# RWKV output stage: two products per token tile are made in the early rounds, parked in DRAM, and loaded when the tile is finished

## The chip, the cores and the metric

The kernel runs on one core of one Trainium2 chip. TensorE (PE) multiplies, VectorE (DVE), ScalarE (ACT) and GpSimd (POOL) work on elements, SyncE (SP) issues most of the DMAs, and ACT and POOL issue some. The metric is the device time of one execution in microseconds (us), as the median of the runs; lower is better.

## The reference, cut to what matters

A two-layer encoder for 512 + 256 = 768 tokens of width 1024. Half of the first layer's mixer is bidirectional RWKV-7 with 8 heads of 64. What is changed computes its last step, for each token, from the two scans' sum `y`:

```
y = scan_forward + scan_backward                          # (tokens, 8 heads, 64)
y = (y - mean(y)) * rsqrt(var(y) + 64e-5)                 # per head
y = y * lnx_w + lnx_b
bonus = sum(r * 0.5 * (k_f + k_b) * r_k) * v              # one number per head and token, times v
out_b = (y + bonus) * g
```

So out_b = yn * (lnx_w * g) + (lnx_b + bonus) * g, where yn is the normalised y. Only yn needs the scans. The result goes, beside the attention half, into the output projection, and from there into the post-norm, the FFN and the second layer.

## The kernel before, in words

The 768 tokens are six tiles of 128 rows (`NT = 6`). `v`, `g`, and the operands of the scan are made first and parked in DRAM (`park`). The scan is cut into chunks of 64 tokens; `Core.rwkv` returns `rounds(lo, hi)`, whose loop variable `n` runs over 24 steps, one chunk of one direction each, forward and backward by turns.

In step `n` the loop fetches step `n+3` (`ahead`: KB, RH, AL, SUV, Ti, all issued by SP), runs `chain` (the part that carries the state S: PE, ACT, PE, ACT and DVE, PE, and two DVE operations on S), and runs `prep` for step `n+2` (PE products, masked by DVE into LR and LK, lines 990 and 1001). When both directions have passed both chunks of a tile, `finish(t)` runs: it is called at n = 10, 11, 14, 15, 22 and 23 for tiles 2, 1, 3, 0, 5 and 4. It loads `v` into `z` (tag gz) and `g` (tag gq), normalises `y`, and applies weight, bias, bonus and gate; PE transposes `z`, and ACT and DVE split it into the operand pair of the output projection. Tags gz and gq have one buffer each; the square of `y` also sits in gq.

Steps 0 to 9 run inside the phase of the differential attention, whose matmuls, softmax and small POOL operations (lines 885 to 887) share the engines with them. Steps 10 to 23 run after it, beside the splitting of the output projection's weights (`wo`: cast on ACT, line 139, difference on POOL, line 140). The output projection follows in `out_and_norm`; its first results need the post-norm's weights (`mix_post`, line 179), which are loaded into space that the recurrence's pool gives back.

The order on each engine isn't written out by hand: a planner puts the instructions in order by priority and by its own simulation, and every queue then runs in that order. `rank(100)` moves `chain` ahead in priority, `rank(-60)` moves `prep` back, and matmuls with operands of type float32r are fillers. A load can be issued long before its place in the program if its buffer is free.

Of the kernel before, what the change touches and what calls it, by code (L numbers as in the profile page):

```python
# [13 lines left out]
ALU = mybir.AluOpType  # L14
# [4 lines left out]
P = 128  # L19
D = 1024  # L20
T = 768
NT = 6
# [32 lines left out]
class Core:  # L55
# [881 lines left out]
    def rwkv(self, rw, park, out):  # L937

        nc, A = self.nc, self.A
        am = []  # L940
        for d in "fb":
            t = rw.tile([P, P], I32, tag="am" + d, name="am" + d)
            nc.scalar.dma_start(t, A["am" + d])
            am.append(t)
        lw, lb = (rw.tile([P, 512], F32, tag=n, name=n) for n in ("lw", "lb"))
        nc.scalar.dma_start(lw, A["lnx_w"].partition_broadcast(P))
        nc.scalar.dma_start(lb, A["lnx_b"].partition_broadcast(P))
        tile = lambda tag, shape, bufs=1: rw.tile(shape, F32, tag=tag, name=self.uid(tag), bufs=bufs)
# [30 lines left out]
        def prep(di, c):  # L979

            u = ready[di, c]
            LK, LR, KBT = (tile(n, [P, 4, 2, 64], NB - 1) for n in ("LK", "LR", "KBT"))
            u["LK"], u["LR"], u["KBT"] = LK, LR, KBT
            KB, RH, AL = (u[n] for n in ("KB", "RH", "AL"))
            st = lambda x, j: x[:, j].rearrange("p s t -> p (s t)")
            b = self.bank("pp")
            for j in range(4):
                self.mm(b[:, j * P:(j + 1) * P], st(KB, j), RH[:, j])
            v = b.bitcast(I32).rearrange("p (j x) -> p j x", x=64)
            nc.vector.tensor_tensor(out=LR.rearrange("p j h x -> p (j h) x").bitcast(I32), in0=v,  # L990
                                    in1=am[di][:, 64:P].unsqueeze(1).to_broadcast([P, 8, 64]), op=ALU.bitwise_and)
            for par in range(2):
                rr = rows[par]
                nc.scalar.copy(out=LK[rr, :, par], in_=AL[rr])
            b = self.bank("pp")
            for j, par in heads:
                self.mm(b[rows[1 - par], j * 64:(j + 1) * 64], KB[rows[par], j, 1 - par], AL[rows[par], j])
            v = b[:, 0:256].bitcast(I32).rearrange("p (j x) -> p j x", x=64)
            for par in range(2):
                rr = rows[par]  # L1000
                nc.vector.tensor_tensor(out=LK[rr, :, 1 - par].bitcast(I32), in0=v[rr],
                                        in1=am[di][rr, 0:64].unsqueeze(1).to_broadcast([64, 4, 64]), op=ALU.bitwise_and)
            b = self.bank("pt")
            for j in range(4):
                self.tr(b[:, j * P:(j + 1) * P], st(KB, j))
            nc.scalar.copy(out=KBT.rearrange("p j h v -> p (j h v)"), in_=b)

        def chain(di, c, first, last):
# [38 lines left out]
                nc.scalar.copy(out=ys[o, c // 2], in_=yb[o])  # L1047
            done.add(c)

        def finish(t):  # L1050

            y = ys[:, t]
            hv = lambda x: x.rearrange("p (h v) -> p h v", h=8)
            bc = lambda x: x.unsqueeze(2).to_broadcast([P, 8, 64])
            st = tile("gst", [P, 3, 8], 2)
            z, q = (tile(n, [P, 512]) for n in ("gz", "gq"))
            nc.sync.dma_start(z, park["v"][t * P:(t + 1) * P])
            nc.vector.tensor_reduce(out=st[:, 0], in_=hv(y), axis=AX.X, op=ALU.add)
            nc.vector.tensor_scalar(out=st[:, 0], in0=st[:, 0], scalar1=1.0 / 64, scalar2=None, op0=ALU.mult)
            nc.vector.tensor_tensor(out=hv(y), in0=hv(y), in1=bc(st[:, 0]), op=ALU.subtract)  # L1060
            nc.scalar.activation(out=q, in_=y, func=AF.Square)
            nc.vector.tensor_reduce(out=st[:, 1], in_=hv(q), axis=AX.X, op=ALU.add)
            self.rpow(st[:, 2], st[:, 1], 1.0 / 64, 64e-5)
            g = tile("gq", [P, 512])
            nc.sync.dma_start(g, park["g"][t])
            nc.vector.tensor_tensor(out=hv(z), in0=hv(z), in1=bc(self.bon[:, t]), op=ALU.mult)
            nc.vector.tensor_tensor(out=z, in0=z, in1=lb, op=ALU.add)
            nc.vector.tensor_tensor(out=hv(y), in0=hv(y), in1=bc(st[:, 2]), op=ALU.mult)
            nc.vector.tensor_tensor(out=y, in0=y, in1=lw, op=ALU.mult)
            nc.vector.tensor_tensor(out=z, in0=y, in1=z, op=ALU.add)  # L1070
            nc.vector.tensor_tensor(out=z, in0=z, in1=g, op=ALU.mult)
            b = self.bank("tr")
            for j in range(4):
                self.tr(b[:, j * P:(j + 1) * P], z[:, j * P:(j + 1) * P])
            out(t, b)
# [4 lines left out]
        def ahead(n):  # L1080
            if n < len(todo):
                fetch(*todo[n])
                fetch_inverse(*todo[n])

        def rounds(lo, hi):
            for n in range(2 * lo, 2 * hi):
                if n == 0:
                    for i in range(3):
                        ahead(i)
                    prep(*todo[0])  # L1090
                    prep(*todo[1])
                di, c = todo[n]
                ahead(n + 3)
                with self.rank(100):
                    chain(di, c, n // 2 in (0, 8), n // 2 in (7, 11))
                if n + 2 < len(todo):
                    with self.rank(-60):
                        prep(*todo[n + 2])
                t = c // 2
                passed[t] = passed.get(t, 0) + 1  # L1100
                if passed[t] == 4:
                    finish(t)
# [248 lines left out]
def body(ctx, tc, A):  # L1351
    nc = tc.nc
    C = Core(ctx, tc, A)
    dp = ctx.enter_context(tc.tile_pool(name="dp", bufs=1, space=DRAM, reuse_waits="tile"))
    park = {}
    for n, shp in (("v", [T, 512]), ("o", [4, P, T]), ("g", [NT, P, 512]), ("AL", [2, 12, P, 4, 64]), ("RH", [2, 12, P, 4, 64]), ("KB", [2, 12, P, 4, 2, 64]),
                   ("Ti", [2, 12, P, 4, 64]), ("x", [NT, P, D]), ("va", [NT, P, 512])):
        park[n] = dp.tile(shp, F32, tag="pk" + n, name="pk" + n)
    C.stats = dp.tile([3, T, 8], F32, tag="stats", name="stats")
    C.vperm = dp.tile([2, T, 256], F32, tag="vperm", name="vperm")  # L1360
# [308 lines left out]
```

## Time and profile before

| | |
|---|---|
| median of 3 runs | 2100.59 us (2097.37 to 2102.23) |
| profiled execution, its own time | 2108.94 us |
| span of that execution, first to last instruction | 2107.1 us |
| busy: PE / DVE / ACT / POOL | 2040.0 / 1393.5 / 904.6 / 867.2 us |
| recurrence beside the attention | about 482 to 597 us |
| recurrence after the attention | about 597 to 697 us |
| last `finish` | 697 to 717 us |
| mean granted clock of TensorE | 0.973 of full speed |

A timeline row gives start, duration, engine, line, operation, output and inputs; in brackets stands how long the engine had been idle before, and what it waited for. A window row gives the busy time of each engine in a stretch (with the count of instructions), the granted clock (1.00 is full speed, 2.4 GHz; 0.50 is 1.2 GHz), the mean busy share of the DMA engines, and GB/s.

### The profile page before, as it was taken

How to read it: one execution, taken by the hardware profiler on the slowest of the kernel's cores; microseconds unless marked ns; L12 is line 12 of the kernel's file. 1: busy time of each engine (PE TensorE's matmuls, PEld its weight loads, DVE VectorE, ACT ScalarE, POOL GpSimd, SP SyncE). 2: the span in 40 equal slices, each digit the busy share in tenths (PEclk: the TensorE clock that was granted, in tenths of full speed). 3: DMA queues.
4: the chain of work that ended last, by engine and by line, in shares of the span. 5: the costliest groups of instructions: out<-in, count | busy, mean ns of one | idle time of the engine just before them, and what ended most of it. 6: DMA issues, size and time to landing. Idle time of an engine off the chain costs nothing. (4 is left out here: it accounts for less than half of the span.)

```text
span 2107.1 us, 33782 instructions
## 1 busy us (share of the span) xinstructions
PE 2040.0 (97%) x13294; PEld 1774.0 (84%) x13294; DVE 1393.5 (66%) x2165; ACT 904.6 (43%) x1703; POOL 867.2 (41%) x819
## 2 busy tenths in 40 slices
PE   7999999999999999999999999999998999999998
PEld 7767777877887788999999998888687999999997
DVE  5456987966579577566666658644568566666665
ACT  5466565367554254433333335222444433333332
POOL 3344332652114137443444535453127435543442
PEclk9999997998999999999999999999899999999999
DMA  4334335114365311211222145221131221211124
GB/s 157 85 76 90 88 80 166 35 34 137 86 184 164 121 74 61 80 61 60 66 85 71 63 147 177 82 82 38 52 110 61 80 80 61 80 61 61 60 80 150
DMA packets 150227, 189.01 MB, mean 90 GB/s; under 512 B 95926, under 2 KB 107784, under 8 KB 150068
## 3 DMA queue, kind: packets, MB, share of 16 engines
q1 hardware_dynamic: 126880, 168.00, 26.1%
q10 hardware_dynamic: 20372, 12.03, 2.0%
q0 software_dynamic: 2816, 6.83, 1.0%
q8 instruction: 104, 1.70, 0.3%
q14 instruction: 55, 0.45, 0.1%
HBM read 150.20 MB, written 36.23 MB: 88 GB/s over the span
## 5 line engine op out<-in xcount | busy, mean ns | idle before, releaser
L83 PE MATMUL gm<-xh,w 128*128 128x384 f32 x864 | 237.2, 338 | 2.9 <-DVE sil L340 2.9
L140 DVE TENSOR_TENSOR wl<-wraw,wh 128x1024 fp32r<-128x1024 f32 (+1 forms) x96 | 131.1, 1366 | 152.7 <-ACT wh L139 150.2
L83 PE MATMUL gm<-T,w 128*128 128x384 f32 x1080 | 212.0, 339 | 6.9 <-DVE w L140 3.0
L83 PE MATMUL gm<-xh,wh 128*128 128x256 f32 (+3 forms) x640 | 207.4, 347 | 0.8 <-ACT pad L503 0.8
L83 PE MATMUL gm<-xl,wh 128*128 128x256 f32 (+3 forms) x640 | 205.7, 346 | 0.0
L83 PE MATMUL gm<-xh,wl 128*128 128x256 f32 (+3 forms) x640 | 204.0, 345 | 0.0
L83 PEld LDWEIGHTS gm<-T,w 128*128 128x128 f32 x1080 | 191.8, 188 | 12.7 <-DVE w L140 4.3
L140 DVE TENSOR_TENSOR w<-S,w 128x512 fp32r<-128x512 f32 x174 | 172.7, 992 | 41.3 <-ACT w L139 31.9
L139 ACT CAST wh<-wraw 128x1024 fp32r<-128x1024 f32 (+1 forms) x103 | 107.5, 1045 | 167.8 <-PE gm L83 104.4
L139 ACT CAST w<-S 128x512 fp32r<-128x512 f32 x174 | 107.8, 621 | 150.7 <-POOL S L299 53.6
L139 ACT CAST w<-wraw 128x512 fp32r<-128x512 f32 x126 | 76.1, 619 | 209.3 <-PE gm L83 139.2
L83 PEld LDWEIGHTS gm<-xh,w 128*128 128x128 f32 x864 | 159.2, 189 | 7.8 <-DVE sil L340 3.5
L83 PE MATMUL sc<-xh,w 128*128 128x384 f32 x544 | 151.3, 339 | 3.5 <-DVE xl L140 2.0
L303 POOL TENSOR_TENSOR S<-wraw,S 128x512 f32<-128x512 f32 x42 | 62.2, 1481 | 204.9 <-DVE w L140 204.9
L83 PE MATMUL gm<-xl,w 128*128 128x384 f32 x432 | 145.8, 338 | 0.0
L140 DVE TENSOR_TENSOR w<-wraw,w 128x512 fp32r<-128x512 f32 x126 | 118.3, 954 | 40.2 <-ACT w L139 39.9
L83 PEld LDWEIGHTS gm<-xh,wh 128*128 128x128 f32 (+1 forms) x640 | 119.2, 193 | 21.5 <-issue 6.1
L83 PEld LDWEIGHTS gm<-xl,wh 128*128 128x128 f32 (+1 forms) x640 | 118.7, 194 | 20.4 <-issue 7.9
L83 PEld LDWEIGHTS gm<-xh,wl 128*128 128x128 f32 (+1 forms) x640 | 118.6, 193 | 20.6 <-issue 7.2
L406 DVE TENSOR_TENSOR acc<-acc,ob 128x512 f32<-128x512 f32 x128 | 87.5, 683 | 64.0 <-PE ob L83 63.0
L358 POOL TENSOR_TENSOR sil<-sil,v 128x384 f32<-128x384 f32 x44 | 46.8, 1065 | 167.1 <-DVE v L340 166.8
L83 PE MATMUL ob<-wl,hh 128*128 128x512 f32 x288 | 113.4, 394 | 0.0
(521 smaller groups left out, 5292.6 us busy)
## 6 DMA issues: line engine op xcount, KB each, us to landing
wraw<-in_gate SPq DMA_DIRECT2D x44, 512.0 KB, 3.4
wraw<-in_down SPq DMA_DIRECT2D x44, 512.0 KB, 3.8
wraw<-in_up SPq DMA_DIRECT2D x40, 512.0 KB, 3.5
wraw<-in_wqk SPq DMA_DIRECT2D x20, 512.0 KB, 3.6
wraw<-in_wo SPq DMA_DIRECT2D x14, 512.0 KB, 3.9
wraw<-in_wrkv SPq DMA_DIRECT2D x12, 512.0 KB, 3.5
KB<-pkKB SPq DMA_DIRECT2D x24, 256.0 KB, 3.3
pkx<-x SPq DMA_DIRECT2D x12, 512.0 KB, 4.7
```

The lines of the kernel that those rows point to most:

```text
L83: return self.nc.tensor.matmul(o, a, b, start=start, stop=stop)
L139: self.nc.scalar.copy(out=hi, in_=x)
L140: (eng or self.nc.vector).tensor_tensor(out=lo, in0=x, in1=hi.bitcast(F32), op=ALU.subtract)
L303: eng.tensor_tensor(out=s2, in0=a12, in1=s2, op=ALU.subtract)
L358: nc.gpsimd.tensor_tensor(out=o, in0=o, in1=a[0], op=ALU.mult)
L406: nc.vector.tensor_tensor(out=accs[t][:, fs], in0=accs[t][:, fs], in1=os[t, f], op=ALU.add)
```

## The change

A new function `gated(t)` is called in steps 4 to 9 for tiles 0 to 5. It loads `v` and `g` of the tile, makes z = (v * bonus + lnx_b) * g and g = g * lnx_w in four DVE operations, and stores both to DRAM from POOL's queue. `finish` loads these two instead of `v` and `g`; three of its DVE operations go (v times bonus, plus bias, and the last multiplication by the gate), and the multiplication by `lnx_w` takes the loaded product. Both functions use tags gz and gq, which keep one buffer each.

```diff
+        def gated(t):
+            z, g = tile("gz", [P, 512]), tile("gq", [P, 512])
+            nc.sync.dma_start(z, park["v"][t * P:(t + 1) * P])
+            nc.sync.dma_start(g, park["g"][t])
+            nc.vector.tensor_tensor(out=hv(z), in0=hv(z), in1=bc(self.bon[:, t]), op=ALU.mult)
+            nc.vector.tensor_tensor(out=z, in0=z, in1=lb, op=ALU.add)
+            nc.vector.tensor_tensor(out=z, in0=z, in1=g, op=ALU.mult)
+            nc.gpsimd.dma_start(park["zg"][t], z)
+            nc.vector.tensor_tensor(out=g, in0=g, in1=lw, op=ALU.mult)
+            nc.gpsimd.dma_start(park["lg"][t], g)
         def finish(t):
...
-            nc.sync.dma_start(z, park["v"][t * P:(t + 1) * P])
+            nc.sync.dma_start(z, park["zg"][t])
...
-            nc.sync.dma_start(g, park["g"][t])
-            nc.vector.tensor_tensor(out=hv(z), in0=hv(z), in1=bc(self.bon[:, t]), op=ALU.mult)
-            nc.vector.tensor_tensor(out=z, in0=z, in1=lb, op=ALU.add)
+            nc.sync.dma_start(g, park["lg"][t])
             nc.vector.tensor_tensor(out=hv(y), in0=hv(y), in1=bc(st[:, 2]), op=ALU.mult)
-            nc.vector.tensor_tensor(out=y, in0=y, in1=lw, op=ALU.mult)
+            nc.vector.tensor_tensor(out=y, in0=y, in1=g, op=ALU.mult)
             nc.vector.tensor_tensor(out=z, in0=y, in1=z, op=ALU.add)
-            nc.vector.tensor_tensor(out=z, in0=z, in1=g, op=ALU.mult)
...
+                if 4 <= n < 4 + NT:
+                    gated(n - 4)
```

## Rows read from the trace of the kernel before

**Rows 1.** Section 1 of the page: busy time, share of span, instructions.

```profile
PE 2040.0 (97%) x13294; PEld 1774.0 (84%) x13294; DVE 1393.5 (66%) x2165; ACT 904.6 (43%) x1703; POOL 867.2 (41%) x819
```

**Rows 2.** Windows, three stretches: PE, PEld, DVE, ACT, POOL, clock, DMA share, GB/s.

```profile
500.00:597.00 97.00, 94.72 (x1300) 79.48 (x1300) 59.42 (x142) 60.30 (x163) 15.85 (x49) 1.00 0.41 115
597.00:680.00 83.00, 75.59 (x1221) 66.52 (x1220) 76.54 (x129) 42.84 (x90) 28.42 (x18) 0.94 0.66 191
680.00:720.00 40.00, 37.43 (x283) 30.32 (x282) 20.16 (x34) 7.18 (x18) 6.18 (x7) 0.99 0.19 59
```

**Rows 3.** View of tile gz: ns min/median/max of one, first and last start.

```profile
L1066 DVE TENSOR_TENSOR gz<-gz,bon x6: 674/681/693, 510.6 to 712.6; 128x512 f32<-128x512 f32 x6
L1067 DVE TENSOR_TENSOR gz<-gz,lb x6: 682/692/2727, 512.8 to 713.3; 128x512 f32<-128x512 f32 x6
L1071 DVE TENSOR_TENSOR gz<-gz,gq x6: 682/691/694, 630.7 to 714.8; 128x512 f32<-128x512 f32 x6
```

**Rows 4.** Timeline of DVE: one of the removed operations.

```profile
638.22 2.73 DVE L1067 TENSOR_TENSOR gz<-gz,lb 128x512 f32<-128x512 f32 x1
```

**Rows 5.** Timeline of POOL beside the first of these.

```profile
638.02 2.37 POOL L140 TENSOR_TENSOR wl<-wraw,wh 128x1024 fp32r<-128x1024 f32 x1
```

**Rows 6.** Timeline of PE, 597 to 680 us: the four longest idle gaps.

```profile
608.46 1.13 PE L84 MATMUL gm<-RH,KB 128*128 128x128 f32 x8 [1.03 <-DMA RH<-pkRH]
...
619.46 0.68 PE L84 MATMUL ob<-SUV,KBT 128*64 128x64 f32 x14 [1.66 <-DVE SUV L1029]
...
649.28 0.33 PE L84 MATMUL sc<-SUV,LK 128*64 128x64 f32 x2 [1.21 <-ACT SUV L1017]
...
665.45 0.65 PE L87 MATMUL tr<-ident,gz 128*128 128x128 f32 x4 [1.17 <-DVE gz L1071]
```

**Rows 7.** Waits, 597 to 672 us: total us, times, longest.

```profile
ACT SUV L1017 <- DVE S L1036: 7.5, 3, 5.1
```

**Rows 8.** Windows of 5 us around the low clock.

```profile
645.00:650.00 5.00, 3.62 (x71) 3.11 (x67) 4.97 (x9) 1.15 (x3) 1.19 (x1) 1.00 0.53 157
650.00:655.00 5.00, 4.73 (x46) 3.95 (x44) 4.86 (x9) 4.23 (x9) 2.58 (x2) 0.66 0.52 150
...
665.00:670.00 5.00, 3.77 (x42) 3.10 (x43) 4.55 (x10) 4.22 (x10) 1.79 (x2) 0.76 0.54 125
670.00:675.00 5.00, 5.00 (x64) 4.66 (x63) 3.42 (x7) 0.79 (x3) 0.13 (x1) 0.55 0.61 178
```

**Rows 9.** Timeline of DVE, the last finish.

```profile
712.61 0.69 DVE L1066 TENSOR_TENSOR gz<-gz,bon 128x512 f32<-128x512 f32 x1 [1.30 <-DMA gz<-pkv]
...
714.07 0.69 DVE L1070 TENSOR_TENSOR gz<-ys,gz 128x512 f32<-128x512 f32 x1
```

**Rows 10.** Timeline of SP's queue: the first gz load, the last, and the post-norm's weights.

```profile
504.64 0.42 SPq L1057 DMA_DIRECT2D gz<-pkv  x1
...
710.00 0.32 SPq L1057 DMA_DIRECT2D gz<-pkv  x1
714.78 0.33 SPq L179 DMA_DIRECT2D mix_post<-in_mix_post  x1
```

**Rows 11.** Timeline of PE, the last two transposes' surroundings.

```profile
709.37 0.60 PE L87 MATMUL tr<-ident,gz 128*128 128x128 f32 x4
...
719.38 0.80 PE L83 MATMUL gm<-wh,xh 128*128 128x512 f32 x1 [2.57 <-DVE xn L236]
```

**Rows 12.** DMA issues: queue, count, KB each, median us to landing.

```profile
pkx<-xr POOLq DMA_DIRECT2D x6, 512.0 KB, 3.1
...
gz<-pkv SPq DMA_DIRECT2D x6, 256.0 KB, 2.7
```

**Rows 13.** Timeline of POOL elsewhere: one store that it issues.

```profile
1271.26 0.68 POOL L1500 DMA_DIRECT2D pkx<-xr  x1 [1.36 <-DVE xr L239]
```

**Rows 14.** Waits, 515 to 597 us, of POOL.

```profile
POOL rz L885 <- DVE dst L884: 37.1, 7, 7.0
```

**Rows 15.** Waits of SP's queue, 500 to 597 us.

```profile
SPq L969 <- PE cb L84: 17.5, 5, 6.1
```

More of the change, by code (lines that the diff above doesn't have):

```diff
@@ L1048, in chain @@
             done.add(c)
+        hv = lambda x: x.rearrange("p (h v) -> p h v", h=8)
+        bc = lambda x: x.unsqueeze(2).to_broadcast([P, 8, 64])
+        def gated(t):
[8 more added lines that the diff above has]
+            nc.gpsimd.dma_start(park["lg"][t], g)
         def finish(t):
             y = ys[:, t]
-            hv = lambda x: x.rearrange("p (h v) -> p h v", h=8)
-            bc = lambda x: x.unsqueeze(2).to_broadcast([P, 8, 64])
             st = tile("gst", [P, 3, 8], 2)
             z, q = (tile(n, [P, 512]) for n in ("gz", "gq"))
-            nc.sync.dma_start(z, park["v"][t * P:(t + 1) * P])
+            nc.sync.dma_start(z, park["zg"][t])
             nc.vector.tensor_reduce(out=st[:, 0], in_=hv(y), axis=AX.X, op=ALU.add)
@@ L1356, in body @@
     for n, shp in (("v", [T, 512]), ("o", [4, P, T]), ("g", [NT, P, 512]), ("AL", [2, 12, P, 4, 64]), ("RH", [2, 12, P, 4, 64]), ("KB", [2, 12, P, 4, 2, 64]),
-                   ("Ti", [2, 12, P, 4, 64]), ("x", [NT, P, D]), ("va", [NT, P, 512])):
+                   ("Ti", [2, 12, P, 4, 64]), ("x", [NT, P, D]), ("va", [NT, P, 512]), ("zg", [NT, P, 512]), ("lg", [NT, P, 512])):
         park[n] = dp.tile(shp, F32, tag="pk" + n, name="pk" + n)
```

## The prediction, made before the change was run

> **What bounds the kernel now.** I read the page's first section, then the windows stretch by stretch, then the timelines of the stretches that the change touches. Over the whole span PE is busy for 2040.0 of 2107.1 us [rows 1], so no edit can win more than PE's idle time where it acts, and what a low clock costs there. The windows part the recurrence into three [rows 2]. From 500 to 597 us, beside the attention, PE is busy 94.72 of 97 us, DVE only 59.42: PE sets the pace, and DVE has 37.6 us to spare. From 597 to 680 us it turns round: DVE is busy 76.54 of 83 us (92%), PE idles 7.4 us, and the granted clock is 0.94. From 680 to 720 us PE is full again with the output projection, but for 2.6 us at its end.
>
> In the middle stretch DVE carries the masks and state updates of the scan, and four of the six `finish` calls. The four longest gaps of PE [rows 6] are 1.03 us for a DMA, 1.66 for a DVE copy, 1.21 for an ACT copy and 1.17 for the last multiplication of a `finish`. That ACT copy itself waits on DVE's state update, up to 5.1 us at once [rows 7]. So most of PE's idle time here ends with something that stood in DVE's queue. After such gaps the clock falls: 0.66, 0.76 and 0.55 in three windows of 5 us [rows 8], which is full speed and half speed (2.4 and 1.2 GHz) mixed; the missing shares are worth 1.70 + 1.20 + 2.25 = 5.15 us of PE.
>
> **The change part by part.** The profiled execution took 2108.94 us (span 2107.1 and 1.8 around it), 8.35 above the median of 2100.59; I make the sum against the profile and carry it over to the median.
>
> *Removed, middle stretch.* Lines 1066, 1067 and 1071 go, at a median of 0.68 to 0.69 us each [rows 3]. The operations are 18, but the first gz load was issued at 504.64 us [rows 10], because its buffer was free, and that tile's lines 1066 and 1067 ran then (the first starts, 510.6 and 512.8 [rows 3]). Four finishes with three operations, less these two, leave ten in 597 to 680 us. Nine at 0.69 and one at 2.73 [rows 4] make 8.9 us off a queue of 76.5. What it is worth in time is less. The floor is 0: PE may find its next wait elsewhere. The ceiling is PE's 7.4 idle plus the clock's 5.15, 12.5 us. Of the four gaps 1.03 of 5.07 us is a DMA's and stays; by that share 5.9 of the 7.4 us hang on DVE. DVE's queue gets 8.9/76.5 = 12% shorter, but it is in order and nearly saturated, so a delay shrinks by more than that share. I take 4 of the 5.9, and 1 of the 5.15 for the clock: -5. What is late next is PE itself: 75.6 of 83 us is work that stays.
>
> A row on the price: the 2.73 us operation started 0.2 us after a POOL subtraction of 2.37 us [rows 4, 5] and ended with it. The Trainium skill (SBUF — State Buffer, Who interferes with whom) says that a VectorE instruction with two SBUF inputs and a GpSimd one that reads SBUF block each other for the whole instruction. By that rule the 2.04 us excess doesn't go with the operation; the next one with two SBUF inputs that stands beside the subtraction pays it. The removed work would then be 6.9 us rather than 8.9, the stretch -4 rather than -5, and the total a microsecond smaller.
>
> *Removed, tail.* In the last `finish` z is loaded at 710.00, as soon as the transpose at 709.37 has freed its buffer [rows 10, 11]; it lands and line 1066 starts at 712.61, 1067 follows, line 1070 starts at 714.07 [rows 9] and ends at 714.76. At 714.78 SP issues the load of the post-norm's weights, which needs that space [rows 10], and 4.6 us later PE resumes, after 2.57 us of idleness that a post-norm operation ends [rows 11]. With the products loaded, line 1070 can follow the landing at once: 1.46 us earlier. Line 1071 of the tile before also goes, so the transpose and the load move up by some 0.7 us. Together 2.1 us; the bounds are 0 (the weight product, now a load needed two operations earlier than the gate was, arrives last) and 2.57 (PE has no more to win). I take -2.
>
> *Added, early stretch.* Six tiles with four DVE operations: 24 at 0.69 = 16.6 us, less the 1.4 us that ran there already, 15.2 us into the 37.6 us that DVE has free [rows 2]. PE is full there, so this is covered unless an operation stands before one that PE needs; if the cover were gone, each could delay the scan by 0.69 us, 15.2 in all. I take +1, nearest to PE's own row: it had other work for all but 2.3 of 97 us.
>
> Twelve stores are issued by POOL; a store of double size holds POOL for 0.68 us [rows 13], so 12 x 0.68 = 8.2 us, beside 15.85 us of work in 97 [rows 2]. POOL runs in order: behind a store that waits for DVE stand the softmax's small operations, which themselves wait 37.1 us for DVE in this stretch [rows 14]. They are late already and PE has other work: 0 in the sum, up to 8.2 uncovered.
>
> Twelve loads go into SP's queue, where the scan's fetches stand. With one buffer each, a tile's loads wait until the stores of the tile before have landed. One turn is 2.7 us for the load [rows 12], 4 x 0.69 of DVE, 0.68 of POOL, and at most 3.1 for landing (512 KB; these are 256) [rows 12]: 9.2 us, six turns 55 us. From 504.6 that ends at about 560, if the planner starts them as early as it started the gz load; if it keeps them at steps 4 to 9, some 545 to 597, a turn still fits a step of about 9 us. I count 0 here and price the case that it doesn't below. In `finish` two loads replace two of the same size.
>
> *Sum.* -5 - 2 + 1 = -6: 2102.9 for the profiled execution, 2094.6 as the median.
>
> **The rivals.** (A) *Hidden.* PE's waits end elsewhere: the DMA engines are 66% busy in the middle stretch against 41% before [rows 2], and one of the four gaps is a DMA's already [rows 6]. For it speaks that the planner reorders everything behind a moved operation, so one gap may be traded for another; against it that DVE or a copy behind DVE ends the other three. Then 0 - 2 + 1 = -1: 2099.6.
>
> (B) *Slower: SP's queue is held.* From the second tile on, `gated`'s loads stand in SP's queue until the stores before them have landed, and behind them stand the fetches of the scan. SP's fetches of RH already wait 17.5 us for buffers that PE frees [rows 15], so they are issued just in time and a hold reaches PE. Five turns at 3.1 us of landing are 15.5 us; with the gains of 7 off that is +8.5, 2109.1. It decides for slower as soon as more than half of it, 7 us plus the 4.2 of the threshold, reaches PE. Against it: the planner knows the landing and can put a load behind the fetches. The Trainium skill (SBUF — State Buffer, the box on VectorE blocking DMA) adds that GpSimd can't write a DMA's descriptors while VectorE copies fp32 within SBUF, and line 1017 is such a copy; the stores would land later by it. No row of before shows a POOL store in this stretch.
>
> (C) *Not early.* If the last two tiles slip past 597 us, eight operations (5.5 us) join the saturated queue; at the stretch's rate (5 of 8.9) that gives back 3.1: -2.9, 2097.7.
>
> (D) *More.* Shorter gaps keep the clock up. Nearly all of PE's 5.9 us and most of the 5.15 come back, -10 - 2 + 0: 2088.6.
>
> **How the numbers follow.** Forecast 0.42 (-3 to -9 us), A 0.22, B 0.18, C 0.05, D 0.13. A measurement of this kernel can't tell less than about 0.2% (4.2 us) from no change, so faster means below 2096.4, slower above 2104.8. Four fifths of the forecast's chance and D lie below: 0.47, and with a little of C 0.48. B gives 0.16 of slower, and A with an unlucky order 0.03: 0.19. The rest, 0.33, is within. The range leaves out the far ends of B and D: 2085.5 to 2107. The forecast's own is 2091.6 to 2097.6.
>
> **What would show it.** Right: from 597 us on, three operations fewer per finish, the four multiplications of `gated` before 597 us at about 0.69 us, PE's idle time from there to the output projection down from 7.4 to some 3 us, the clock windows near 1.00, and PE's 2.57 us gap at the end nearly gone. Wrong: SP or POOL waiting on gz or gq with PE idle before 597 us (B); a middle stretch as long as before with DVE less busy (A); gated operations after 597 us (C).

## The result: slower by 0.7%, and the profile after

The kernel after takes 2117.7 us (median of five runs, 2110.5 to 2120.3), the kernel before 2101.1 in the same comparison: a ratio of 1.0072, 95% interval 1.0047 to 1.0097. The forecast was 2094.6 with a range of 2085.5 to 2107. It had the wrong sign, and the measured time lies above the range. The profiled execution took 2119.49 us, with a span of 2117.7, which is 10.6 us longer than the span of before. (The median of before was between 2101.1 and 2105.4 us in this comparison and the five told below; every ratio is against runs of before on the same chip in the same comparison.)

The busy times of the page, which answer to [rows 1]:

```profile
PE 2039.0 (96%) x13294; PEld 1773.9 (84%) x13294; DVE 1391.4 (66%) x2171; ACT 905.1 (43%) x1703; POOL 876.4 (41%) x831
```

PE has the same work and is busy for a microsecond less, and its mean granted clock is 0.973 in both executions. So over the whole span the 10.6 us are idle time of PE. The windows that answer to [rows 2] (PE, PEld, DVE, ACT, POOL, clock, DMA share, GB/s) show where:

```profile
500.00:597.00 97.00, 93.51 (x1210) 77.16 (x1210) 69.34 (x156) 57.47 (x153) 23.77 (x58) 0.96 0.59 173
597.00:680.00 83.00, 66.61 (x1042) 58.14 (x1041) 65.84 (x107) 39.99 (x85) 29.29 (x21) 0.90 0.64 187
680.00:730.00 50.00, 50.00 (x537) 42.12 (x534) 22.14 (x44) 9.58 (x23) 4.95 (x5) 1.00 0.19 56
```

Up to 597 us PE got through 1210 matmuls, 90 fewer than before, and its clock fell. From 597 to 680 it idled 16.4 us, not 7.4. DVE was no longer full there either: 65.8 of 83 us, not 76.5. From 680 on PE never stopped.

The early rounds ran before 597 us, where the forecast put them, and their multiplications took the 0.69 us that it gave. A turn was slower than it had it: five turns from 509.4 to 574.8 us are 13.1 us each, not 9.2. The first of the four operations in the view of tile gz, which answers to [rows 3] (ns min/median/max of one, first and last start):

```profile
L1058 DVE TENSOR_TENSOR gz<-gz,bon x6: 673/692/693, 509.4 to 574.8; 128x512 f32<-128x512 f32 x6
```

PE's idle gaps over 1 us from 590 to 735 us, which answer to [rows 6] and, since none comes near the end, to [rows 11]:

```profile
601.50 0.44 PE L87 MATMUL tr<-ident,o 128*128 128x128 f32 x2 [1.50 <-DVE o L922]
607.95 0.33 PE L84 MATMUL sc<-SUV,KBT 128*64 128x64 f32 x2 [1.55 <-ACT SUV L1029]
617.68 0.70 PE L84 MATMUL sc<-SUV,LK 128*64 128x64 f32 x15 [3.32 <-ACT SUV L1017]
621.70 0.51 PE L84 MATMUL sc<-Xs,Ti 64*64 64x64 f32 x10 [1.79 <-ACT Xs L1022]
629.49 1.12 PE L84 MATMUL ob<-SUV,LK 128*64 128x64 f32 x16 [4.36 <-DVE LK L1001]
...
663.20 1.31 PE L84 MATMUL gm<-RH,KB 128*128 128x128 f32 x8 [1.44 <-DMA RH<-pkRH]
```

Five of the six, with 12.5 of their 14.0 us, lie between 600 and 630 us, before the first shortened `finish` has given PE anything. I call this place the seam: the attention has just ended, its result comes back as the operand of the output projection, eight weights of that projection are loaded and split, and the recurrence goes on from step 10. Three of these five gaps end with a copy of the recurrence on ScalarE. What stood ahead of those copies is in ScalarE's timeline (start, us, and in brackets the idle time before and what ended it):

```profile
611.03 0.83 ACT L139 CAST xh<-wraw 128x768 fp32r<-128x768 f32 x1 [2.87 <-DMA wraw<-pko]
...
613.52 0.83 ACT L139 CAST xh<-wraw 128x768 fp32r<-128x768 f32 x1 [1.18 <-DMA wraw<-pko]
616.28 1.04 ACT L139 CAST wh<-wraw 128x1024 fp32r<-128x1024 f32 x1 [1.92 <-DMA wraw<-in_wo]
617.23 0.40 ACT L1017 COPY SUV<-S 64x256 f32<-64x256 f32 x1
```

The copy at 617.23 for which PE waits 3.32 us stands right behind a cast that itself waits 1.92 us for a weight still being loaded. On VectorE the order has changed too. First the kernel before, then the kernel after (L922 is the attention's last output, L1036 a state update, L1045 a step's output, L140 the subtraction of a split):

```profile
593.00 0.42 DVE L922 TENSOR_TENSOR o<-ob,drs 128x256 f32<-128x256 f32 x1
593.96 0.69 DVE L1045 TENSOR_TENSOR ys<-ys,cb 64x512 f32<-64x512 f32 x1 [0.54 <-PE cb L84]
599.02 1.83 DVE L140 TENSOR_TENSOR xl<-wraw,xh 128x768 fp32r<-128x768 f32 x2 [0.90 <-ACT xh L139]
603.67 0.42 DVE L1036 TENSOR_TENSOR S<-S,dc 128x256 f32<-128x256 f32 x1
604.85 0.69 DVE L1045 TENSOR_TENSOR ys<-ys,sc 64x512 f32<-64x512 f32 x1 [0.75 <-PE sc L84]
606.95 0.95 DVE L140 TENSOR_TENSOR xl<-wraw,xh 128x768 fp32r<-128x768 f32 x1
```

```profile
599.42 0.69 DVE L1045 TENSOR_TENSOR ys<-ys,cb 64x512 f32<-64x512 f32 x1 [1.11 <-PE cb L84]
601.02 0.42 DVE L922 TENSOR_TENSOR o<-ob,drs 128x256 f32<-128x256 f32 x1
606.93 1.83 DVE L140 TENSOR_TENSOR xl<-wraw,xh 128x768 fp32r<-128x768 f32 x2 [2.09 <-ACT xh L139]
611.89 0.96 DVE L140 TENSOR_TENSOR xl<-wraw,xh 128x768 fp32r<-128x768 f32 x1 [1.31 <-ACT xh L139]
614.39 0.96 DVE L140 TENSOR_TENSOR xl<-wraw,xh 128x768 fp32r<-128x768 f32 x1 [1.53 <-ACT xh L139]
615.83 0.42 DVE L1036 TENSOR_TENSOR S<-S,dc 128x256 f32<-128x256 f32 x1
616.61 0.69 DVE L1045 TENSOR_TENSOR ys<-ys,sc 64x512 f32<-64x512 f32 x1
```

Before, two subtractions come, then step 10's state update and output, then the other two; the attention's last output stands ahead of step 9's output. After, step 9's output comes first, and all four subtractions stand ahead of step 10's state update. Call these the old and the new order. From the attention's last output to step 10's output it is 11.85 us before and 15.6 after. The diff touches none of these lines: the planner placed them otherwise because instructions had moved elsewhere.

The tail did what was forecast. The last operation of the last `finish` (DVE), and SP's loads about it, which answer to [rows 9, 10]:

```profile
725.05 0.69 DVE L1081 TENSOR_TENSOR gz<-ys,gz 128x512 f32<-128x512 f32 x1 [1.29 <-DMA gz<-pkzg]
```

```profile
722.44 0.32 SPq L1070 DMA_DIRECT2D gz<-pkzg  x1
725.77 0.33 SPq L179 DMA_DIRECT2D mix_post<-in_mix_post  x1
```

From the load of the last tile to the load of the post-norm's weights it is 3.33 us where it was 4.78: 1.45 earlier, and the forecast worked out 1.46. PE's 2.57 us gap behind it is gone.

### The profile page after: what moved, and what is told of

It reads as the page before. It is cut to its first block, busy times and chain, and to the rows that moved or that the text cites. A ratio compares the mean times of both kernels' runs of the same rounds, so it can differ in the third digit from the quotient of the medians.

```text
span 2117.7 us, 33839 instructions
## 1 busy us (share of the span) xinstructions
PE 2039.0 (96%) x13294; PEld 1773.9 (84%) x13294; DVE 1391.4 (66%) x2171; ACT 905.1 (43%) x1703; POOL 876.4 (41%) x831
## 5 line engine op out<-in xcount | busy, mean ns | idle before, releaser
L140 DVE TENSOR_TENSOR wl<-wraw,wh 128x1024 fp32r<-128x1024 f32 (+1 forms) x96 | 127.3, 1326 | 157.4 <-ACT wh L139 154.3
L140 DVE TENSOR_TENSOR w<-S,w 128x512 fp32r<-128x512 f32 x174 | 170.3, 979 | 40.8 <-ACT w L139 33.3
L140 DVE TENSOR_TENSOR w<-wraw,w 128x512 fp32r<-128x512 f32 x126 | 117.8, 950 | 38.9 <-ACT w L139 38.8
```

What stands on the lines that cost most here:

```text
L140: (eng or self.nc.vector).tensor_tensor(out=lo, in0=x, in1=hi.bitcast(F32), op=ALU.subtract)
```

## The experiments

Eighteen kernels. Theory S: the order of work at the seam costs the time. Theory W: the work of the early rounds does. Theories L, C and O, told where they come in, part the inside of the seam.

To compare the profiled executions I use three landmarks: the first Xs copy of the forward recurrence (498.9 us in the kernel before), the start of the attention's last output on VectorE (593.0), and SP's load of the post-norm's weights (714.8). The stretch before the first varies from 492.8 to 499.1 us among the executions, and the one behind the last is 1387 to 1395 us in all of them, whatever the kernel; so the two parts between them hold what was changed. The last landmark doesn't stand behind the same work of PE in all of them (2795 matmuls after the first landmark in the kernel before, 2769 in the kernel after), since a finish that ends sooner leaves some of the output projection behind it. The column "equal work" therefore gives the time from the first landmark to the 3600th matmul after it, which lies in the FFN. The table is the key to what follows:

| kernel | rounds at steps | order | to attention's end | from there on | sum | equal work | ratio to before, 95% interval |
|---|---|---|---|---|---|---|---|
| before | none | old | 94.1 | 121.8 | 215.9 | 384.7 | 1 |
| after | 4 to 9 | new | 102.4 | 124.8 | 227.2 | 397.8 | 1.0072 [1.0047, 1.0097] |
| after_s0 | 0 to 5 | old | 95.9 | 116.3 | 212.2 | 380.2 | 1.0004 [0.9990, 1.0017] |
| before_free | none | old | 93.7 | 123.4 | 217.1 | 385.4 | 1.0007 [0.9993, 1.0021] |
| after_free | 4 to 9 | old | 100.7 | 118.2 | 218.9 | 387.7 | 1.0009 [0.9996, 1.0022] |
| add_s0 | 0 to 5, unused | old | 96.8 | 123.8 | 220.6 | 388.2 | 1.0014 [0.9998, 1.0029] |
| e1_add | 4 to 9, unused | new | 104.5 | 133.3 | 237.8 | 405.7 | 1.0108 [1.0092, 1.0125] |
| e2_remove | none | new | 95.5 | 123.5 | 219.0 | 387.9 | 1.0006 [0.9992, 1.0019] |
| before_seam | none | new | 97.7 | 128.3 | 226.0 | 392.2 | 1.0058 [1.0037, 1.0078] |
| before_late | none | casts moved | 93.7 | 143.6 | 237.3 | 405.1 | 1.0084 [1.0063, 1.0105] |
| before_once | none | casts in one row | 93.9 | 124.0 | 217.9 | 386.8 | 1.0028 [1.0016, 1.0040] |
| after_once | 4 to 9 | casts in one row | 98.9 | 126.4 | 225.3 | 392.5 | 1.0037 [1.0021, 1.0054] |

In the new order the first part holds one output of the recurrence more, so only the sum and the equal work are compared across the two orders. The equal work of the kernels before and after as windows (same fields as [rows 2]; the counts agree to within one or two matmuls at the edges):

```profile
498.85:883.55 384.70, 365.18 (x3602) 319.08 (x3603) 271.22 (x438) 189.13 (x418) 128.20 (x144) 0.97 0.38 115
```

```profile
498.57:896.37 397.80, 369.33 (x3602) 321.64 (x3601) 274.56 (x444) 189.02 (x418) 136.93 (x156) 0.97 0.41 127
```

That is 13.1 us more, of which 9.0 are idle time of PE.

### First four: the halves of the change, and its place

**e1_add.** The rounds are kept, the tile's end is that of before.

```diff
+                if 4 <= n < 4 + NT:
+                    gated(n - 4)
 ...
         def finish(t):   # lines 1055 to 1077 as before
```

> The added part alone: gated(t) runs in steps 4 to 9 and stores its two products, and finish is as it was before (it loads v and g and makes all its products itself). In DVE's order all four subtractions of the attention's operand split (line 140, xl from wraw) stand ahead of the state update of step 10, as in the changed kernel. Theory S (the seam: the loss comes from that order, because DVE and ACT stand waiting for the attention's last output on its way through DRAM while the scan's step 10 is ready behind them): slow, 2115 to 2121 us, with about 10 us of PE idle time in the 30 us after the attention's last output, and without the gain at the end. Theory W (the added work delays attention and scan in the early stretch, and the loss grows with it): slow as well, 2112 to 2120.

2124.8 us, ratio 1.0108 and above the ranges of both theories, so it doesn't part them. Adding alone, in the new order, makes 1.1%; against the kernel after (2117.7) the shorter tile's end is then worth 7 us by the medians, 7.9 by the equal work.

**e2_remove.** The reverse: the shortened end, with v and g loaded in place of the products, which nobody makes.

```diff
-            nc.sync.dma_start(z, park["zg"][t])
+            nc.sync.dma_start(z, park["v"][t * P:(t + 1) * P])
-            nc.sync.dma_start(g, park["lg"][t])
+            nc.sync.dma_start(g, park["g"][t])
 ...
-                if 4 <= n < 4 + NT:
-                    gated(n - 4)
```

> The removed part alone: no gated; finish has the three operations fewer and loads v and g where the changed kernel loads the two products, so the output is not the reference's. In DVE's order all four subtractions of the attention's operand split stand ahead of the state update of step 10, as in the changed kernel and unlike the kernel before. Theory S: not faster than before in spite of the smaller work: 2103 to 2113 us, with 8 us or more of PE idle time after the attention's last output. Theory W: faster than before by the gain that was forecast, 2091 to 2097, since no work is added.

2104.3 us, ratio 1.0006, within S's range and above W's. Taking eighteen operations away, ten of them in VectorE's fullest stretch, gained nothing, and this kernel came out in the new order too. So the flip doesn't need the added work. That the order ate the gain is likely from the pairs below, but this run alone doesn't show it.

**after_s0.** All of the change, one number different: the rounds are made at steps 0 to 5.

```diff
-                if 4 <= n < 4 + NT:
-                    gated(n - 4)
+                if 0 <= n < 0 + NT:
+                    gated(n - 0)
```

> The changed kernel with gated in steps 0 to 5 instead of 4 to 9: the same work. In DVE's order two of the four subtractions stand behind the state update of step 10, as in the kernel before. Theory S: most of the loss is gone, 2094 to 2104 us, PE idle time after the attention's last output 5 us or less. Theory W: as slow as the changed kernel or slower, 2112 to 2120, since the same work lies in the early stretch.

2103.8 us, ratio 1.0004, within S's range: 14 us under the kernel after with the same instructions. It has the old order. That speaks for S, and against W in the form that the work alone costs the time.

**after_pool.** The subtractions that stood ahead of the state update go to GpSimd.

```diff
-        C.split(xh[:, j], xl[:, j], C.raw(park["o"][j], T)[:, :T])
+        C.split(xh[:, j], xl[:, j], C.raw(park["o"][j], T)[:, :T], nc.gpsimd)
```

> The changed kernel with the four subtractions of the attention's operand split on POOL instead of DVE, so that no state update stands behind them on DVE; ACT's four casts still wait for the same loads. Theory S: faster than the changed kernel by 5 to 12 us, 2103 to 2112, the rest of the loss staying with ACT. Theory W: within 3 us of the changed kernel, 2114 to 2121.

2114.7 us, ratio 1.0061 [1.0044, 1.0079], where S gave 2103 to 2112: a miss, and within W's range. Step 10's state update was early again (604.9 us), and no more than 3 us came back, which the intervals can't tell from nothing. So the subtractions on VectorE are not, by themselves, what costs. ScalarE still stood in casts, whose waits for loads were 12.7 us from 590 to 640 us, against 10.2 in the kernel after.

### The order by itself, on unchanged work

**before_seam.** The kernel before; the splits of the attention's operand get a higher rank, which turns the order.

```diff
     for j in range(4):
-        C.split(xh[:, j], xl[:, j], C.raw(park["o"][j], T)[:, :T])
+        with C.rank(150):
+            C.split(xh[:, j], xl[:, j], C.raw(park["o"][j], T)[:, :T])
```

> The kernel before, all its work and none of the change's, with one edit: the splits of the parked attention operand are given a higher rank, so that all four subtractions stand on VectorE ahead of step 10's state update, as they do in the kernel after (and their casts on ScalarE ahead of the recurrence's copies). Theory S (the order of work at the seam costs the time): 2112 to 2119 us, with 8 us or more of TensorE idle between 595 and 630 us. Theory W (the added work itself costs it): 2100 to 2105 us, as nothing is added here.

2115.2 us, ratio 1.0058 [1.0037, 1.0078], within S's range and far above W's. PE was idle for only 3.9 us between 595 and 630 us, where S gave 8 or more, so the time came as S had it and the place only in part. Nothing of the change is in this kernel, and it loses as much as the kernel after, to within the intervals.

**after_late, before_late, remove_late.** The kernels after, before and e2_remove, with two weights of the output projection split ahead of the last two quarters of the attention's operand.

```diff
-    for j in range(4):
+    for j in range(2):
         C.split(xh[:, j], xl[:, j], C.raw(park["o"][j], T)[:, :T])
-    W = wo(0, 8, extra.enter_context(C.pool("xw0")))
+    xw0 = extra.enter_context(C.pool("xw0"))
+    W = wo(0, 2, xw0)
+    for j in range(2, 4):
+        C.split(xh[:, j], xl[:, j], C.raw(park["o"][j], T)[:, :T])
+    W += wo(0, 8, xw0, 2)
```

> The kernel after, with its six early rounds (steps 4 to 9) unchanged; only the first two weights of the output projection are split ahead of the last two quarters of the attention's operand, so that those two stand behind step 10's state update. Theory S: 2096 to 2106 us, 10 us or more under the kernel after. Theory W: 2113 to 2120 us, since all the work is still there at the same steps.

> The control to after_late: the kernel before with that same change of order (two weights ahead of the last two quarters) and nothing else. Both theories: 2098 to 2105 us, as its subtractions already stood apart. The distance from it to after_late is the change's effect with the seam mended: Theory S: -5 to +2 us; Theory W: +10 us or more.

> Only the removal (the shortened tile's end, which loads v and g in place of the products; the products are left out, so the output is not the reference's), with the seam mended as in after_late. Theory S: the removal is worth what the prediction gave the middle and the tail, 4 to 8 us: 2093 to 2099 us. Theory N (the shorter tile's end is hidden whatever the seam does): 2100 to 2105 us.

2114.7, 2122.4 and 2108.6 us (ratios 1.0053 [1.0035, 1.0072], 1.0084 [1.0063, 1.0105], 1.0022 [1.0010, 1.0034]). Every absolute expectation failed but W's for after_late: my mended order was a worse one, and it hit the control hardest. The distance is still of use: under this arrangement the kernel after is 8 us faster than the kernel before, where W wanted 10 us slower and S between 5 faster and 2 slower. And before_late is the cleanest case of what order costs. Its two parts by the landmarks:

```profile
493.10:586.80 93.70, 91.94 (x1239) 76.97 (x1240) 58.59 (x140) 59.82 (x163) 16.84 (x50) 1.00 0.42 116
586.80:730.40 143.60, 125.61 (x1556) 106.63 (x1555) 99.59 (x163) 48.98 (x102) 30.87 (x22) 0.89 0.42 120
```

The first part is that of before_free (below) in length and in PE's busy time. The second is 20 us longer with the same work: PE idles 18.0 us, and the clock is 0.89. ScalarE shows casts that wait for weights (wh casts 10.5 us in all from 586 to 640 us, at most 4.6 at once), with the recurrence's copies behind them, as here:

```profile
602.82 1.05 ACT L139 CAST wh<-wraw 128x1024 fp32r<-128x1024 f32 x1 [1.63 <-DMA wraw<-in_wo]
603.77 0.40 ACT L1017 COPY SUV<-S 64x256 f32<-64x256 f32 x1
```

PE, idle for 2.23 us, goes on at 604.22, behind this copy.

### The change with the order at the seam held

**after_free and before_free.** The four loads of the attention's operand read an input instead, so they never wait for the attention's store.

```diff
-        C.split(xh[:, j], xl[:, j], C.raw(park["o"][j], T)[:, :T])
+        C.split(xh[:, j], xl[:, j], C.raw(A["wo0"][j][:, 0:T], T)[:, :T])
```

> The kernel after, rounds at steps 4 to 9 as they are, but the four loads of the parked attention operand read the same amount from an input instead (the output is not the reference's), so they never wait for the attention's last store. With that, the subtractions fall back to the order of the kernel before: two, then step 10's state update, then two. Theory S: 2096 to 2106 us, 10 us or more under the kernel after, with no work taken away. Theory W: 2111 to 2118 us.

> The control to after_free: the kernel before with the same four loads from an input (its order of subtractions does not change). Both theories: 2096 to 2103 us. Its distance to after_free is the change with the order held: Theory S: -4 to +4 us; Theory W: +10 us or more.

2106.3 and 2106.9 us: with both in the old order at the seam, and the rounds at steps 4 to 9 as the change has them, it makes no difference. Both medians lie a little above S's ranges (by 0.3 and 3.9 us), and the distance between them is S's. W falls. But the zero is a sum. The two parts, first of before_free, then of after_free, the later part up to equal work:

```profile
493.90:587.60 93.70, 91.94 (x1240) 76.97 (x1240) 58.61 (x140) 59.73 (x163) 16.99 (x50) 1.00 0.40 108
587.60:879.30 291.70, 270.15 (x2366) 238.92 (x2364) 212.06 (x299) 128.86 (x255) 110.42 (x94) 0.98 0.36 114
```

```profile
496.30:597.00 100.70, 97.22 (x1239) 80.18 (x1239) 72.24 (x161) 60.24 (x163) 26.61 (x62) 0.97 0.55 163
597.00:884.00 287.00, 268.78 (x2366) 237.93 (x2364) 201.38 (x283) 129.28 (x255) 111.39 (x94) 0.98 0.37 115
```

For the same 1240 matmuls the early part takes 7.0 us more: 1.7 of idle PE, and 5.3 of longer busy time, of which the clock (0.97 over 100.7 us) makes 3.0; where the other 2.3 come from is open. The later part takes 4.7 us less for the same 2366 matmuls, 3.3 of it idle time of PE (5.2 less up to the last landmark, as the table has it). Where the early loss begins, in after_free: the stretch of 20 us in which the clock falls, PE's gaps over half a microsecond there, VectorE's and POOL's rows ahead of them:

```profile
516.30:526.30 10.00, 8.40 (x100) 6.25 (x100) 8.75 (x18) 6.56 (x15) 3.42 (x4) 0.78 0.62 175
526.30:536.30 10.00, 10.00 (x97) 8.54 (x93) 7.49 (x18) 4.81 (x12) 2.62 (x7) 0.88 0.48 143
```

```profile
519.70 0.44 PE L87 MATMUL tr<-ident,o 128*128 128x128 f32 x2 [0.98 <-DVE o L922]
521.01 0.68 PE L84 MATMUL cb<-SUV,LK 128*64 128x64 f32 x14 [0.62 <-DVE SUV L1017]
```

```profile
514.19 2.52 DVE L856 TENSOR_TENSOR l<-k,k 64x768 fp32r<-64x768 f32 x1
...
517.60 1.59 DVE L1036 TENSOR_TENSOR S<-S,dc 128x256 f32<-128x256 f32 x1
519.22 0.42 DVE L922 TENSOR_TENSOR o<-ob,drs 128x256 f32<-128x256 f32 x1
519.56 0.68 DVE L1058 TENSOR_TENSOR gz<-gz,bon 128x512 f32<-128x512 f32 x1
...
520.67 0.29 DVE L1017 COPY SUV<-S 64x256 f32<-64x256 f32 x1
```

```profile
511.15 0.67 POOL L1061 DMA_DIRECT2D pkzg<-gz  x1 [0.25 <-DVE gz L1060]
511.85 1.12 POOL L157 TENSOR_TENSOR drs<-var,mh 128x2 f32<-128x2 f32 x1
512.94 0.59 POOL L1063 DMA_DIRECT2D pklg<-gq  x1
...
514.10 1.81 POOL L856 TENSOR_TENSOR q<-q,q 64x768 fp32r<-64x768 f32 x1
```

The two stores hold POOL for 0.67 and 0.59 us among the small operations of the attention: from the first of these to the start of the subtraction behind them it is 3.5 us (510.6 to 514.1), where it is 2.1 in before_free (508.2 to 510.3). That subtraction, POOL's own of L856, now begins with VectorE's second. That one takes 2.52 us, where it takes 0.94 in before and in before_free; the state update behind it and the attention's output are late, and a multiplication of `gated` stands ahead of the SUV copy for which PE waits 0.62 us. That is 1.6 us of PE; then the granted clock falls to 0.78 and 0.88 for 20 us, which at full speed is 3.4 us of PE's work. This chain is read from the rows and not tested: no run issued the stores from another engine. Nor is the order held in this stretch. In before_free the attention's output stands ahead of both subtractions on VectorE (509.45, then 509.90 and 513.40 us); in after_free it stands behind them. So the 7.0 us are the price of the added work in the place that the planner gave it. The Trainium skill (SBUF — State Buffer, Who interferes with whom) has VectorE with two inputs in SBUF and a GpSimd instruction that reads SBUF block each other. These rows agree: POOL's subtraction ends at 515.91, and VectorE's, begun at 514.19, ends 0.80 us behind that.

**add_s0.** Adding alone, in the old order (e1_add with its rounds at steps 0 to 5).

```diff
-                if 4 <= n < 4 + NT:
-                    gated(n - 4)
+                if 0 <= n < 0 + NT:
+                    gated(n - 0)
```

> Adding alone in the good order: the early rounds at steps 0 to 5 are made and stored, the tile's end is that of the kernel before (nothing of the products is used). Work of 24 VectorE operations, 12 loads and 12 stores on top of the kernel before. Theory S with the working of the prediction (early rounds nearly hidden): 2102 to 2106 us. Theory A (the early rounds cost 6 us or more on their own, and the removal gives that back): 2108 to 2114 us, 5 us or more above the kernel with the whole change at the same steps (2103.8).

2107.5 us, ratio 1.0014 [0.9998, 1.0029], between the two ranges. At these steps the first part is 2.7 us longer than in the kernel before, not 7. Against after_s0 the removal takes 7.5 us off the later part (123.8 to 116.3), or 7.1 by the equal work.

**s0_free.** after_s0 with the loads of after_free; here they turn the order to the new one.

> The whole change with its rounds at steps 0 to 5, and the four loads from an input; here that turns the order the other way, all four subtractions ahead of step 10's state update, though nothing waits for the attention any more (the output is not the reference's). Theory S as a matter of order alone: 2110 to 2118 us. Theory S as a matter of the wait for data (the casts hold ScalarE only because their data is late): 2098 to 2106 us. Theory W: 2101 to 2106 us.

2118.8 us, ratio 1.0072 [1.0050, 1.0094]: nearest to S as a matter of order, 0.8 us above its range and 12 or more above the others. Nothing waits for the attention's store in it, and its loss is that of the kernel after. So the late operand is not needed for the loss; the order, taken as a whole, is enough.

### Inside the seam

Theory L: the casts' waits for their loads. Theory C: the casts' place ahead of the copies on ScalarE. Theory O: the place of the attention's last output.

**after_raw4, before_raw4.** Four raw buffers in place of two.

```diff
+        r = xr.tile([P, 1024], F32, tag="xraw", name=C.uid("xraw"), bufs=2)
+        nc.sync.dma_start(r[:, :w], src)   # every second operand
```

> The kernel after (rounds at steps 4 to 9), with four raw buffers in place of two for the attention operand and the eight weights of the output projection; the four subtractions still stand in one row ahead of step 10's state update. Theory L (the casts' waits for their loads hold ScalarE and with it the recurrence): 2100 to 2108 us, and ScalarE's waits for loads between 590 and 640 us fall from 10 us to under 4. Theory O (the place of the subtractions and casts alone): 2112 to 2119 us. Theory W: 2113 to 2119 us.

> The control to after_raw4: the kernel before with four raw buffers. Its four subtractions too now come ahead of a state update. Theory L: 2098 to 2106 us. Theory O: 2110 to 2117 us. Theory W: 2098 to 2104 us.

2113.4 and 2107.5 us (1.0041 [1.0026, 1.0056], 1.0010 [0.9996, 1.0024]). The first is above L's range and within those of O and W, the second in the gap between all of them. ScalarE's waits for loads from 590 to 640 us fell from 10.2 to 6.1 us, where L wanted under 4, and at most 4 us of 12 or more came back (2 by the equal work, 395.9 us). L has a part at most, not the whole. before_raw4, with its four subtractions in one row too but the attention's last output in its old place, lost nothing that can be told.

**after_once, before_once.** One weight is loaded once and split twelve times.

```diff
+    r0 = C.raw(A["wo0"][0])
-        C.split(xh[:, j], xl[:, j], C.raw(park["o"][j], T)[:, :T])
+        C.split(xh[:, j], xl[:, j], r0[:, :T])   # and the eight weights from r0 as well
```

> The kernel after, but one weight is loaded once and split into all twelve places (the output is not the reference's): casts and subtractions are all there, the loads are not, so no cast waits for one. Theory L: 2094 to 2104 us. Theory W: 10 us or more above before_once.

> The control to after_once: the kernel before with one weight loaded once and split into all twelve places. Both theories: 2094 to 2103 us. The distance from it to after_once is the change without the loads of the seam: Theory L: -6 to +3 us; Theory W: +10 us or more.

2113.2 and 2111.4 us (1.0037 [1.0021, 1.0054], 1.0028 [1.0016, 1.0040]). L's absolute numbers fail: with no load to wait for, both are slower than the kernel before. ScalarE's timeline of before_once has seven casts in one row, 5.8 us, and the recurrence's copies behind them:

```profile
598.25 3.03 ACT L139 CAST xh<-wraw 128x768 fp32r<-128x768 f32 x4
601.18 2.94 ACT L139 CAST xwh<-wraw 128x1024 fp32r<-128x1024 f32 x3
604.02 0.36 ACT L1029 COPY SUV<-sc 64x256 f32<-64x256 f32 x1
```

The distance of the two is 1.8 us, within L's range and against W again. But here the later part is not shorter in the kernel after (the table has 126.4 against 124.0 us, and at equal work 293.7 against 292.9), so what the removal wins isn't the same under every order.

**after_pc, before_pc.** The operand's four casts and subtractions go to GpSimd.

```diff
-        C.split(xh[:, j], xl[:, j], C.raw(park["o"][j], T)[:, :T])
+        o = C.raw(park["o"][j], T)[:, :T]
+        nc.gpsimd.tensor_copy(out=xh[:, j], in_=o)
+        nc.gpsimd.tensor_tensor(out=xl[:, j], in0=o, in1=xh[:, j].bitcast(F32), op=ALU.subtract)
```

> The kernel after, rounds at steps 4 to 9, with the four casts and subtractions of the attention operand on GpSimd instead of ScalarE and VectorE; the attention's last output still stands where it stands in the kernel after. Theory C (casts in front of the recurrence's copies in ScalarE's queue): 2098 to 2108 us, with no idle time of TensorE over 2 us on a ScalarE copy between 600 and 620 us. Theory O (place of the attention's last output): 2112 to 2118 us.

> The control to after_pc: the kernel before with the same four casts and subtractions on GpSimd. Theories C and O: 2096 to 2106 us. The distance from it to after_pc is the change with these casts out of the way: Theory C: -5 to +4 us; Theory O: +8 us or more.

2112.9 and 2102.9 us (1.0037 [1.0024, 1.0051], 0.9989 [0.9975, 1.0003]). C fails: about 5 us came back, and 10 remain between the two. O's number holds, but O isn't shown by it, since the early part also differs (101.3 us to the attention's end, against 96.4).

**What stays open.** That the order alone can cost as much as was lost is shown: before_seam and before_late without any of the change, after_s0 against s0_free with all of it (s0_free's other loads cost nothing in before_free). Which instruction of the order costs it is not shown. Every kernel with the full work and the attention's last output behind step 9's output loses 0.4 to 1.1%; taking from it the subtractions, the operand's casts or half of the waits gives back 3 to 5 us each by the medians, which is about what the intervals can tell. But before_late and before_once lose in the old place too. No version was found that is faster than the kernel before by more than can be told. Buffers of their own for the loads of `gated`, and another engine for its stores, were not tried.

## Why the prediction was wrong

At equal work the kernel after is 13.1 us longer than the kernel before. The free pair and the order part it: early rounds +7.0, removal -4.7, order at the seam +10.1 (397.8 against after_free's 387.7), and 0.7 for what before_free differs from before. (By the sums, which end at unequal work, it is 11.3: +7.0, -5.2, +8.3 and 1.2.) These are single profiled executions, so a microsecond or two of each term can be noise. The forecast had +1, -7 and no term for order.

**The step that failed most: the order was taken as given.** The prediction worked out what leaves a queue and what enters one, and let the rest stand where it stood. It did say under rival A that "the planner reorders everything behind a moved operation, so one gap may be traded for another", and priced that at 0, as a trade within one stretch. The runs put 8 to 10 us (profiles) or 13 us (the ratio of after_free, 1.0009, to that of after, 1.0072) in its place, more than any term of the sum. Removal alone turned the order as well. One row pointed to the place: by [rows 6] one of PE's four long gaps already ended with a copy of the recurrence on ScalarE, so what stands ahead of such copies could reach PE.

**"I take +1, nearest to PE's own row."** The early rounds cost 7.0 us at steps 4 to 9 in the free pair, 5 in the pair before_once and after_once, and about 2 to 3 at steps 0 to 5. The bound of 15.2 held; the value was too small. The term beside it, POOL's stores, "0 in the sum, up to 8.2 uncovered", is the one that the rows above speak against: the stores took 0.54 to 0.67 us each, as worked out from [rows 13], but the waits of [rows 14] were no full cover. By the chain read there they push POOL's subtraction beside VectorE's, and the attention's output, for which PE waits, stands behind that. The sum also had no price for a lower clock: 3.4 us of PE's work went to it behind 1.6 us of gaps in that one place.

**Removed, middle and tail: near, where the seam had the old order.** Forecast -5 and -2, together -7; measured at equal work -4.7 (free pair) and -7.1 (at steps 0 to 5), of which idle time of PE makes 3.3 and 5.3: the mechanism that was forecast. The tail's 1.46 us came as 1.45, and its gap went. That DVE is relieved shows in its 201.4 us of the later part against 212.1. In the pair before_once and after_once PE's idle time in that part falls by 4.7 us as well, but its busy time grows by 5.5, and nothing is won.

**The rivals.** B named the side, and with 2109.1 came nearest, by another mechanism. SP's waits from 500 to 597 us, which answer to [rows 15]:

```profile
SPq L1056 <- DMA pkzg<-gz: 6.6, 3, 4.7
SPq L1070 <- DMA pkzg<-gz: 4.9, 1, 4.9
...
SPq L1057 <- DMA pklg<-gq: 2.3, 1, 2.3
```

That is 8.9 us for `gated` and 4.9 for the first `finish`, together 13.8 where B had 15.5; but no gap of PE in that stretch ended with a DMA, so by this trace the hold was there and didn't reach PE. (B's own threshold was also summed wrongly: 7 + 4.2 is 11.2 of 15.5, nearly three quarters of it and not "more than half".) C did not happen: the last round began its multiplications at 574.8 us. A and D fell with the order. The chance for slower, 0.19, held 0.03 for "A with an unlucky order". An unlucky order is the larger part of what came, and it had a chance but no price. One row was also read a little off: VectorE's 2.73 us operation of [rows 4] ended 0.56 us behind POOL's subtraction, and not with it.

## What to carry to other kernels

Where a planner places the instructions, a moved operation has two prices: its own, which can be worked out from the rows, and that of the order which comes out, which here was larger. The same work in another order was 0.6 to 0.8% slower in three cases (before_seam, before_late, and s0_free against after_s0), and no order was found that is faster by more than can be told. To know what an edit does, run it in two orders, or make a control that comes out in the same order, and look at the order of both; a version that moves only the step at which the work is done is the cheapest. Small operations and DMA issues on a nearly idle engine need not be free when that engine lies on the way to something PE waits for; here that is read from the rows, not tested. And where a landmark inside a trace ends a comparison, count the matmuls up to it in both kernels.

## What the runs showed of the hardware

A short idle time of PE can cost about twice itself behind it, and need not. In after_free 1.6 us of gaps around 520 us were followed by granted clocks of 0.78 and 0.88 in windows of 10 us (full and half speed mixed). In after_pc the same two gaps (0.95 and 0.62 us, at 517.7 and 519.0) were followed by none: its granted clock is 1.00 up to the attention's end. VectorE's 64x768 subtraction took 0.94 us alone and 2.52 beside a GpSimd subtraction of 1.81 us. A cast of 128x1024 took 1.04 us on ScalarE. Its wait for the load of a weight in two buffers was 0.9 to 1.9 us in four casts of the kernel after and 1.6 to 4.6 in four of before_late, so there the waits weighed more than the work; in the kernel before the one such wait was 0.8 us. The kernel before itself spread from 2097.6 to 2111.8 us over 29 runs of one comparison, while the stretch up to the attention's end took 93.7 to 94.1 us in five of the six kernels that add nothing to it and keep the old order: landmarks inside a trace tell apart what whole runs can't.
